# Second attention of a two-layer hybrid backbone: the next group's row maxima start seven score tiles after the group's start instead of four

## The chip, the cores and the metric

The kernel runs on one core of one Trainium2 chip. The metric is the device time of one execution in microseconds, lower is better. The profiles come from the hardware profiler, one execution each.

## The reference

The model is a two-layer backbone over 1024 latent tokens (a grid of 16 rows by 64 columns) and 256 context tokens, model width 1024, everything in fp32. Layer 0 has global and windowed attention. Layer 1, in which the change lies, has a convolution module and a neighbourhood attention with 8 heads of 64. Each query row of the grid sees the 256 context keys and a band of 8 rows by 16 columns, with a bias table for the relative position:

```python
bias = jnp.concatenate([ctx_open, bias], axis=-1)[None, :, None]
kk = jnp.concatenate([c_dk, kr], axis=1)
vv = jnp.concatenate([c_dv, vr], axis=1)
return gqa_attend(qr[:, :, :, None, :], kk, vv, bias).reshape(bsz, GRID_W, D_W)
```

`gqa_attend` is a softmax attention: scores, bias, softmax over the keys, product with the values. The result is gated with a SiLU, joined with the convolution's result, multiplied by an output matrix, added to the residual, and normalised.

## The kernel before

All matrix products are computed to nearly fp32 accuracy in three passes: each operand is split into a high part (`ph`, `wh`, `hh`) and a low part (`pl`, `wl`, `hl`); line 325 makes the high part (a cast on ACT), line 328 the low part (POOL or DVE), and lines 347 to 349 are the three matmuls.

The second attention handles 16 groups, g0 to g15. A group is one head and one half of the grid's columns, 512 queries. Heads 0 to 5 have their two halves one after the other; the last four groups are head 6 half 0, head 7 half 0, head 6 half 1, head 7 half 1. A group has seven score tiles: one of 128 context keys, five of the band (128 to 384 queries wide), and another of 128 context keys. Per tile:

- L503 and L507: two matmuls write the scores `st` (two PSUM banks). The first multiplies the queries' high part `QH` by the keys `KAt`; the second multiplies `QL` by `KBt`. Rows 64 to 67 of `QL` hold the negated row maxima of the four query blocks, so that the second matmul also subtracts the maximum.
- L512 (DVE) adds the bias `bs`, L513 (ACT) takes the exponential; for the context tiles L515 (ACT) does it alone. L325 and L328 split the result.
- L445 to L447: three matmuls, run three tiles later (`flush`), accumulate values and denominators in `ov`, of which there is one PSUM bank.

When the last tile of a group has been flushed, that is at tile 2 of the next group, DVE normalises: L455 (transpose), L457, L458, L1451 (`y` from `ov`; with it the bank is free) and L1453 (`y` times the gate). For heads 0 to 5 the result goes to DRAM (L1457), and comes back as `od` for the output projection; heads 6 and 7 stay on the chip.

Each group needs a preparation (`attn_prep`), a Python generator:

- its first step loads QH, QL and the bias for the maxima, `bm`, through SP's queue (L1382, L1383, L1385);
- six steps compute the row maxima: L1424 (matmuls against the context keys, two into one bank) with L1426 (a reduction on DVE), twice, and L1432 (a matmul against the band's keys) with L1435 (add the bias and take the maximum, on DVE), four times, in two banks `mx`;
- the seventh step reduces them (L405), two empty steps follow, and the tenth transposes the maxima (L415, PE) and writes them into QL (L416, DVE).

The first step of group g+2's preparation is taken at the first tile of g, and the rest is put into a list `work` with a due position, `x + LEAD[1]`, where x counts score tiles over all groups. From that position on, `prepare` takes `g.rate` = 3 steps a tile for each entry in the list, but only of the first entry while it lasts: half of them before the tile's flush, the rest after it. A dictionary changes the rule at the end: g11 takes up no preparation, g12 takes up those of g13 and g14, g13 that of g15. Before a group's first tile, whatever is left of its own preparation is run to its end:

```python
while any(p is g.prep for _, p in work):
    prepare(len(items), 1)
for k in g.ids:
    next(preps[k])
    work.append((x + LEAD[layer[0]], preps[k]))
```

The keys of the next head (`KAt`, 768 KB) are loaded through SP's queue at the start of a head's first half (L389), and ACT copies 64 of their rows to `KBt` at the end of that group (L593).

Beside the attention runs other matrix work, woven in as steps (`weave`): the projections of heads 4 to 7 (`d_proj`, matmuls `p`, whose results ACT and DVE evict, among them `vT`, `vc`, `sgd`, `spk`, `spq`, and `trv` are transposes of the values), then the output projection of the convolution's part (`po<-oc`), then that of the attention's part (`po<-od`), and the end of the kernel. These steps have a priority somewhat ahead of the attention's.

The order on each engine is then set by a planner: it simulates the program in time with costs of its own, and gives each engine, of the instructions that are ready in its simulation, the one that is first in the generators' order, corrected by the priorities. So an instruction that stands later may be placed earlier where an engine would have been free. On the chip each engine follows its list strictly in order.

Of the kernel before, what the change touches and what calls it, by code (L numbers as in the profile page):

```python
# [31 lines left out]
KROWS = ((0, 8), (0, 11), (4, 15), (8, 16))  # L32
BMO = (0, 320, 320, 760)
LOOK0, LOOK1 = 3, 3
LEAD = (3, 4)
AHEAD = 3
BSW, BMW = 768, 1080
CWB = 12
# [62 lines left out]
def tile_kernel(ctx: ExitStack, tc: tile.TileContext, a, out):  # L101
# [326 lines left out]
    def attn_gen(pool, groups, vshare, look, nexts=None):  # L428
# [58 lines left out]
        for x, (g, t) in enumerate(items):  # L487
            if x + AHEAD < len(items):
                items[x + AHEAD][0].ahead(items[x + AHEAD][1])
            if t == 0:  # L490
# [3 lines left out]
# [3 lines that stand above are left out]
            rate = g.rate * max(len(work), 1)  # L497
# [1305 lines left out]
```

## Time and profile before

| | |
|---|---|
| median of 3 runs | 1508.71 us (1506.60 to 1510.68) |
| profiled execution, its own time | 1508.76 us |
| span in its profile | 1506.7 us |
| mean granted TensorE clock | 0.977 |
| busy share: PE, weight loads, DVE, ACT, POOL | 95%, 77%, 72%, 50%, 54% |

The profile names engines as follows: PE is the matmul engine and PEld its weight loads, DVE the vector engine, ACT the activation engine, POOL GpSimd, SP the engine that issues most transfers. An instruction is shown by its start, its length, engine, line, operation, and output<-inputs. Square brackets hold the time in which the engine was idle before it, and what it waited for. A granted clock of 1.00 is full speed. In the second attention's stretch PE has the two longest waits at the row maxima of g4 and g8, whose queries are still on their way.

### The profile page before, as it was taken

Reading aid. Unit: us, or ns where it says so; the run is one execution under the profiler, and the core shown is the slowest. Engines: PE = TensorE matmul, PEld = TensorE weight load, DVE = VectorE, ACT = ScalarE, POOL = GpSimd, SP = SyncE. Lnnn points to the kernel's source line nnn. Section 1 sums busy time; section 2 is a strip of 40 time slices with the busy share of each in tenths; the row PEclk is TensorE's granted clock in tenths of the full one; section 3 lists DMA queues with packets and bytes.
Section 4 is the critical chain, followed back from the end, with each engine's and each line's share of the span. In section 5 each row is a group of like instructions: output and inputs, shape, how many; then the busy total and the mean of one; then the engine's idle time right before and its main releaser. Section 6 shows DMA issues by size and latency. Waiting matters only on the chain.

```text
span 1506.7 us, 22055 instructions
## 1 busy us (share of the span) xinstructions
PE 1424.8 (95%) x7006; PEld 1164.5 (77%) x7006; DVE 1086.2 (72%) x2139; ACT 750.3 (50%) x1536; POOL 816.9 (54%) x764
## 2 busy tenths in 40 slices
PE   7699999999999999999999989999999999999996
PEld 2598887987788678778888768888887878788775
DVE  5996787589957677555477676999938466677766
ACT  3541344446454765665455665443434354555563
POOL 3261463466555686776455765764543343364663
PEclk9799999999999999999999989999999999999998
DMA  9766245424541123641111122212596777797523
GB/s 351 261 201 190 73 123 179 144 67 122 161 133 47 45 84 119 218 156 45 49 42 43 60 77 80 86 65 69 160 315 197 209 219 209 231 292 219 189 63 119
DMA packets 182827, 215.23 MB, mean 143 GB/s; under 512 B 17196, under 2 KB 136184, under 8 KB 182712
## 3 DMA queue, kind: packets, MB, share of 16 engines
q1 hardware_dynamic: 176048, 202.26, 43.2%
q10 hardware_dynamic: 6664, 11.57, 2.4%
q8 instruction: 55, 0.90, 0.2%
q14 instruction: 60, 0.49, 0.1%
HBM read 151.64 MB, written 62.13 MB: 142 GB/s over the span
## 4 chain that ended last, share of the span: by engine, by line
PE 71%; DVE 13%; DMA 8%; issue 3%; POOL 2%; ACT 1%; SPq 1%; DVEq 0%; ACTq 0%; POOLq 0%
PE p L347 6%; PE p L348 6%; PE p L349 6%; PE ov L445 5%; PE ov L447 4%; PE ov L446 4%; PE po L347 4%; PE po L349 4%; PE po L348 4%; PE st L507 4%; PE st L503 4%; DMA mw<-in_mod_w_dram 3%; PE pg L347 2%; PE pq L349 2%; PE pq L347 2%
## 5 line engine op out<-in xcount | busy, mean ns | idle before, releaser
L328 POOL TENSOR_TENSOR pl<-pf,ph 128x512 fp32r<-128x512 f32 (+3 forms) x321 | 392.4, 1233 | 257.3 <-ACT ph L325 208.0
L328 POOL TENSOR_TENSOR wl<-wr,wh 128x256 fp32r<-128x256 f32 (+2 forms) x253 | 194.5, 787 | 160.5 <-ACT wh L325 112.4
L515 ACT ACTIVATE pf<-st 128x512 f32<-128x512 f32 x284 | 166.6, 596 | 179.6 <-PE st L507 129.9
L325 ACT CAST ph<-pf 128x512 fp32r<-128x512 f32 (+3 forms) x364 | 205.8, 578 | 24.0 <-PE ov L446 13.3
L347 PE MATMUL p<-hh,wh 128*128 128x512 f32 x448 | 177.6, 398 | 2.4 <-ACT wh L325 1.6
L348 PE MATMUL p<-hl,wh 128*128 128x512 f32 x448 | 178.0, 399 | 0.0
L349 PE MATMUL p<-hh,wl 128*128 128x512 f32 x448 | 173.1, 396 | 0.0
L325 ACT CAST wh<-wr 128x256 fp32r<-128x256 f32 (+2 forms) x260 | 101.6, 405 | 128.9 <-DMA wr<-in_od_d_dram 39.7
L445 PE MATMUL ov<-ph,Vt 128*128 128x512 f32 (+3 forms) x364 | 141.8, 390 | 10.1 <-DVE y L669 6.4
L503 PE MATMUL st<-QH,KAt 128*128 128x512 f32 (+3 forms) x364 | 139.7, 385 | 6.4 <-ACT pf L515 4.1
L447 PE MATMUL ov<-pl,Vt 128*128 128x512 f32 (+3 forms) x364 | 142.2, 392 | 3.7 <-DVE pl L328 1.9
L446 PE MATMUL ov<-ph,Vt 128*64 128x512 f32 (+3 forms) x364 | 139.5, 383 | 0.0
L507 PE MATMUL st<-QL,KBt 68*128 68x512 f32 (+3 forms) x364 | 135.6, 382 | 1.2 <-DVE QL L416 1.2
L1200 DVE SCALAR_TENSOR_TENSOR cps<-U,taps,cps 128x512 f32<-128x512 f32 x184 | 124.4, 749 | 0.1
L627 DVE TENSOR_REDUCE mp<-mx 128x1 f32<-128x512 f32 x128 | 85.6, 684 | 37.8 <-PE mx L626 37.1
L347 PEld LDWEIGHTS p<-hh,wh 128*128 128x128 f32 x448 | 84.5, 189 | 22.8 <-ACT wh L325 2.2
L349 PEld LDWEIGHTS p<-hh,wl 128*128 128x128 f32 x448 | 84.4, 188 | 20.1 <-issue 0.5
L348 PEld LDWEIGHTS p<-hl,wh 128*128 128x128 f32 x448 | 84.5, 189 | 19.0 <-issue 0.2
L447 PEld LDWEIGHTS ov<-pl,Vt 128*128 128x128 f32 x364 | 71.1, 195 | 27.6 <-POOL pl L328 5.1
L445 PEld LDWEIGHTS ov<-ph,Vt 128*128 128x128 f32 x364 | 71.4, 196 | 25.7 <-issue 6.1
L347 PE MATMUL pq<-wh,hh 128*128 128x384 f32 x256 | 88.0, 344 | 0.0
L349 PE MATMUL pq<-wh,hl 128*128 128x384 f32 x256 | 87.5, 342 | 0.0
(289 smaller groups left out, 3443.0 us busy)
## 6 DMA issues: line engine op xcount, KB each, us to landing
mw<-in_mod_w_dram SPq DMA_DIRECT2D x34, 512.0 KB, 5.9
Q<-qs SPq DMA_DIRECT2D x40, 256.0 KB, 2.6
QH<-Q SPq DMA_DIRECT2D x80, 128.0 KB, 2.8
bm<-in_d_bm_dram SPq DMA_DIRECT2D x16, 540.0 KB, 5.4
wr<-in_od_d_dram SPq DMA_DIRECT2D x64, 128.0 KB, 2.8
mw<-in_mod_w_dram SPq DMA_DIRECT2D x28, 256.0 KB, 3.0
wr<-in_ev_qkv_dram SPq DMA_DIRECT2D x32, 192.0 KB, 4.5
QD<-spq SPq DMA_DIRECT2D x48, 128.0 KB, 2.5
```

Source lines behind the costliest of these rows:

```text
L325: SC.copy(hi, src)
L328: (GP if leng == "g" else VE).tensor_tensor(lo, src, hi.bitcast(F32), op=ALU.subtract)
L347: PE.matmul(o, lh, rh, start=first, stop=False)
L348: PE.matmul(o, lh, rl, start=False, stop=False)
L349: done[0] = PE.matmul(o, ll, rh, start=False, stop=last)
L445: PE.matmul(o, V[:, 64:192], ph, start=(t == 0), stop=False)
L446: PE.matmul(cut(g.ov[0:64], q0, n), V[:, 0:64], ph, start=False, stop=False)
L447: pvs.append(PE.matmul(o, V[:, 64:192], pl, start=False, stop=(last and g.sink is None)))
L503: sts.append(PE.matmul(sf, KA[:, cs], cut(g.QH, q0, n), start=True, stop=False))
L507: PE.matmul(sf, KB[0:68, cs], cut(g.QL[0:68], q0, n), start=False, stop=True)
L515: SC.activation(pf[:, :n], st[:, :n], AF.Exp, scale=1.0 if g.bias else SCALE)
L1200: VE.scalar_tensor_tensor(pc, uc, w, pc, op0=ALU.mult, op1=ALU.add)
```

## The change

One constant: the second entry of `LEAD`, used in the second attention alone, goes from 4 to 7, the number of tiles in a group. The first attention's stays 3.

```diff
-LEAD = (3, 4)
+LEAD = (3, 7)
```

## Prediction before the run

> **What bounds the kernel now.** I read the page first, for the engines and the chain that ended last.
>
> ```profile
> span 1506.7 us, 22055 instructions
> PE 1424.8 (95%) x7006; PEld 1164.5 (77%) x7006; DVE 1086.2 (72%) x2139; ACT 750.3 (50%) x1536; POOL 816.9 (54%) x764
> PE 71%; DVE 13%; DMA 8%; issue 3%; POOL 2%; ACT 1%; SPq 1%; DVEq 0%; ACTq 0%; POOLq 0%
> ```
>
> PE is busy 95% of the span and holds 71% of the chain. The change adds and removes no instruction, so it can only pay by taking away or making idle time of PE (and the slow clock behind it). The stretch of the second attention, 1180 to 1440 us, by length and busy time (PE, its weight loads, DVE, ACT, POOL, then granted clock, DMA share and GB/s):
>
> ```profile
> 1180.00:1440.00 260.00, 246.01 (x1263) 206.28 (x1262) 179.64 (x443) 138.25 (x307) 123.69 (x141) 0.97 0.72 220
> ```
>
> PE idles 260.0 - 246.0 = 14 us of it; nothing larger than that is to be won by order alone, but for the clock. Next, PE in order of time: the idle in brackets stands ahead of the instruction. The rows are the two largest waits, what follows each, the start of some groups (g3 at 1236.52, g7 at 1315.35, g13 at 1412.91, g14 at 1431.83; g0 to g15 are the sixteen groups of seven tiles), and the late waits.
>
> ```profile
> 1228.16 0.47 PE L1424 MATMUL mx<-KAt,QH 128*128 128x256 f32 x2 [2.85 <-DMA QH<-QD]
> 1229.37 0.69 PE L1322 MATMUL trv<-ident,vc 128*128 128x128 f32 x2
> 1236.52 0.40 PE L503 MATMUL st<-QH,KAt 128*128 128x512 f32 x1
> 1296.93 0.71 PE L1424 MATMUL mx<-KAt,QH 128*128 128x256 f32 x2 [2.91 <-DMA QH<-QD]
> 1298.45 0.63 PE L347 MATMUL p<-hh,wh 128*128 128x512 f32 x1
> 1315.35 0.39 PE L503 MATMUL st<-QH,KAt 128*128 128x512 f32 x1
> 1389.41 0.47 PE L445 MATMUL ov<-ph,Vt 128*128 128x512 f32 x1 [0.61 <-DVE y L1451]
> 1412.91 0.40 PE L503 MATMUL st<-QH,KAt 128*128 128x512 f32 x1
> 1415.60 0.73 PE L347 MATMUL po<-od,wh 128*128 128x512 f32 x2 [1.14 <-ACT od L325]
> 1417.78 0.84 PE L507 MATMUL st<-QL,KBt 68*128 68x512 f32 x2
> 1425.45 0.40 PE L1424 MATMUL mx<-KAt,QH 128*128 128x256 f32 x2
> 1431.83 0.39 PE L503 MATMUL st<-QH,KAt 128*128 128x512 f32 x1
> 1437.10 0.69 PE L503 MATMUL st<-QH,KAt 128*128 128x384 f32 x1 [1.81 <-DVE pf L512]
> 1443.84 0.40 PE L507 MATMUL st<-QL,KBt 68*128 68x512 f32 x1
> ```
>
> Two waits of 2.85 and 2.91 us are row maxima, the moved step itself, whose queries QH have not landed. The chain that ended last passes through both transfers:
>
> ```profile
> 1220.25 7.78 DMA QH<-QD
> ...
> 1290.35 6.45 DMA QH<-QD
> ```
>
> The stretches around these waits and near the end of the attention, in the same columns:
>
> ```profile
> 1228.20:1232.00 3.80, 3.80 (x16) 3.39 (x17) 2.21 (x5) 2.73 (x8) 3.14 (x4) 0.57 1.06 389
> 1297.00:1302.00 5.00, 5.00 (x17) 4.26 (x18) 3.37 (x7) 3.32 (x8) 1.98 (x2) 0.66 1.05 334
> 1416.00:1420.00 4.00, 4.00 (x14) 3.23 (x13) 1.80 (x4) 2.13 (x6) 2.65 (x3) 0.57 0.73 245
> 1430.00:1441.00 11.00, 8.44 (x41) 6.69 (x39) 10.15 (x25) 6.68 (x16) 5.76 (x7) 0.82 0.37 113
> ```
>
> After each wait PE runs at about half clock for some microseconds, and the transfer engines are full. Who else waits there? ACT:
>
> ```profile
> 1226.55 1.47 ACT L593 CAST KBt<-KAt 64x1536 fp32r<-64x1536 f32 x1 [3.45 <-DMA KAt<-KD]
> 1228.97 0.35 ACT L1304 COPY vc<-p 128x256 f32<-128x256 f32 x1
> ...
> 1294.89 1.47 ACT L593 CAST KBt<-KAt 64x1536 fp32r<-64x1536 f32 x1 [4.20 <-DMA KAt<-KD]
> 1297.07 0.42 ACT L1309 COPY vT<-p 128x320 f32<-128x320 f32 x1
> ```
>
> This second waiter decides the size of the gain: ACT stands at the next head's keys, loaded with the same burst, until 1226.55 and 1294.89, then copies for 1.47 us, and only then come the exponentials and evictions that free PE's next work.
>
> **The change part by part.** The moved step holds, per group, these DVE instructions (busy, mean ns):
>
> ```profile
> L1435 DVE CUSTOM_DVE_ANT_0 mx<-mx,bm 128x440 f32<-128x440 f32 (+1 forms) x60 | 33.0, 560 | 22.9 <-PE mx L1432 22.4
> L1426 DVE TENSOR_REDUCE mp<-mx 128x2 f32<-128x512 f32 x29 | 19.8, 684 | 3.9 <-PE mx L1424 3.7
> L416 DVE TENSOR_TENSOR QL<-trn,k_bd 4x512 fp32r<-4x512 f32 x16 | 10.9, 682 | 0.5
> ```
>
> That is 4 x 0.560 + 2 x 0.684 + 0.682 = 4.3 us of DVE, and some short ones, beside eight maxima matmuls and one transpose on PE. It issues no DMA: the loads of QH, QL and the bias come at the group's first tile as before, so SP and POOL are moved past nothing, except that the bias load of g15 now waits for the maxima of g13 in SP's queue; behind it stands the gate load of g13, whose use is a group away, so I cost it at nothing.
>
> In the generator's order the ten calls of a preparation fell at tiles 4, 5 and 6 (three each) of group g and the last at tile 0 of g+1. With seven they start at tile 0 of g+1, where two preparations are queued and the rate is six: all six maxima calls at tile 0, the rest at tile 1. Around g11 and g12 it differs: g12 is prepared alone (three calls a tile, tiles 0 to 3 of g11), g13 falls due only when g13 itself starts, so its whole preparation is run ahead of its first score tile, and g15's runs over tiles 0 to 3 of g14.
>
> 1. Gain at the two waits. g4's maxima move from within g2 to g3's start, from 1228.16 to about 1236.5, and QH landed at 1220.25 + 7.78 = 1228.03; g8's move from 1296.93 to about 1315.4, landed at 1296.80. Both transfers are then early by 8 and 18 us. Gross this is 2.85 + 2.91 = 5.76 us, and the clock behind: 3.8 x 0.43 + 5.0 x 0.34 = 3.3 us; upper end 9.1. What is late next is ACT. At 1228 the work between the wait and the transpose (1229.37 - 1228.16 = 1.2 us) could run inside the gap, but the transpose needs vc, which ACT ends at 1229.32. At 1297 the work until the projection (1298.45 - 1296.93 = 1.5 us) fits in the gap, but the projection needs a bank that the vT copy frees at 1297.49, so it comes some 1.0 us earlier. Lower end 1.2 + 1.0 = 2.2. I take -4.0, nearer the lower end, since ACT's rows are the nearer ones and the gap that stays keeps the slow clock.
>
> 2. Gain at g11's result. DVE's order in g12:
>
> ```profile
> 1406.38 0.62 DVE L1435 CUSTOM_DVE_ANT_0 mx<-mx,bm 128x440 f32<-128x440 f32 x1
> ...
> 1407.03 0.69 DVE L1426 TENSOR_REDUCE mp<-mx 128x2 f32<-128x512 f32 x1
> 1407.75 1.78 DVE L1453 SCALAR_TENSOR_TENSOR y<-y,gt 64x512 f32<-64x512 f32 x1
> ```
>
> g13's maxima stand between the pieces of g11's result y, 1407.75 - 1406.38 = 1.37 us of them right ahead of its last one. That result goes to DRAM and back as od, for which PE idles 1.14 us at 1415.60, then runs four microseconds at 0.57, 1.7 us lost. Without them: 0 to -2.9. I take -1.1, the wait alone, because g13's maxima may still be fetched forward.
>
> 3. g13's bunched preparation.
>
> ```profile
> 1414.42 0.68 DVE L416 TENSOR_TENSOR QL<-trn,k_bd 4x512 fp32r<-4x512 f32 x1
> ...
> 1434.64 0.68 DVE L416 TENSOR_TENSOR QL<-trn,k_bd 4x512 fp32r<-4x512 f32 x1
> ```
>
> Before, g13's maxima row was written by 1415.10, and the first score that needs it ran at 1417.78. The quickest nearby preparation is g15's, from 1425.45 to 1435.32: 9.9 us. Begun only at g13's first score (1412.91), it ends at 1422.8, 5.0 us after 1417.78. But the planner fetches work forward where an engine is free, so with DVE's 4.3 us alone it would be in time. 0 to +5.0; I take +1.5.
>
> 4. g15. Its preparation takes 9.9 us, and g14, in which it now lies, has from 1431.83 to 1443.84, where g15's row is needed: it just fits. But DVE is busy 10.15 of 11 us there and PE already waits 1.81 us for it; two maxima operations that ran before 1430 come in, 0.68 + 0.56 = 1.2 us. 0 to +3.0 (they come in, and the 1.81 is had once more); I take +1.0, near the 1.2.
>
> 5. The crowd at the start of a group. The 4.3 us of DVE now stand at tiles 0 and 1, right ahead of the previous group's normalisation at tile 2, which frees the one ov bank. One wait for it stands in the trace, 0.61 us at 1389.41. Over 13 boundaries 0 to +7.9, and below nothing by that 0.61 if the old place was its cause. I take +1.0.
>
> Sum: -4.0 - 1.1 + 1.5 + 1.0 + 1.0 = -1.6. The profiled execution took 1508.76 us (span 1506.7 and 2.1 around it), beside a median of 1508.71, so the time comes to 1507.1.
>
> Term 1 rests on the clock. The rows show half clock after waits of 2.85 and 2.91 us. "TensorE: Matmul & The Clock Gate", Part 1, of the Trainium skill has the clock halve after at least one idle window of about 3.4 us; by its length alone these gaps would cost no clock, the upper end of term 1 would be 5.76 and the sum no other, since I take 4.0. The rows of this case disagree with that reading and decide.
>
> **The rivals.** A: the planner, with the maxima out of the way, lays other ready work under the key loads, and both gaps go with their slow clock: -9.1 in place of -4.0, so 1508.8 - 9.1 - 1.1 + 3.5 = 1502.1. For it: PE has projection work right behind (1298.45). Against: ACT's own wait remains. B: the ov bank. The crowd delays the normalisation at every boundary as at 1389.41: +7.9 in place of +1.0, 1514.0, slower. It decides from 0.55 us a boundary: 13 x 0.55 = 7.1 in place of +1.0 puts the sum above +4.5. Against: DVE is free 28% of the span. C: g13's row is late by the full 5.0 us and the clock falls, 1.7 more as after the wait at 1415.60: 1507.1 + 5.2 = 1512.3, about at the bound. D: the planner's forward fetching puts the maxima back near their old place, and the time stays 1508.7.
>
> **How the numbers follow.** A difference under 0.3% (4.5 us) can't be told from none here. Forecast and D together 0.39, A 0.34, B 0.15, C 0.12. A ends under 1504.2, B above 1513.2, C half above it: faster 0.34, same 0.39 + 0.06 = 0.45, slower 0.21; as a new order can draw a new stall of the size of those seen (2.9 us and its clock, twice), I move 0.06 from same to slower. The range goes from 1499.5 (A without the 3.5 of terms 3 to 5 would be 1498.6) to 1514.0 (B). The likeliest case's own range is 1504 to 1511.
>
> **What would show it.** Step 1: no row-maxima matmul waits for QH; ACT still waits for the keys at L593, and PE has shorter gaps at the same places. Step 2: g11's y ends earlier against g12's first score and PE's wait for od shrinks. Step 3: a wait on QL or its transpose ahead of g13's scores. Step 4: more than 1.81 us of PE waits for DVE in g14. Step 5: more waits of ov for y. The prediction is wrong if the gaps at the key loads vanish altogether, or if the score tiles from g12 on are stretched by more than 5 us.

## The result and the profile after

The changed kernel is slower: 1514.16 us at the median against 1507.35 us for the kernel before in the same session, a ratio of 1.0037 [1.0020, 1.0053]. Two repeats gave 1.0036 [1.0015, 1.0057] and 1.0037 [1.0022, 1.0052]. The forecast was no change, 1507.1 us. The profile shown here is that of the first repeat (its own time 1515.06 us), as the execution that was profiled with the first result ran at about half the granted clock throughout. Its page:

```profile
span 1513.3 us, 22060 instructions
...
PE 1425.0 (94%) x7006; PEld 1161.3 (77%) x7006; DVE 1086.3 (72%) x2139; ACT 749.2 (50%) x1536; POOL 814.6 (54%) x764
...
PE 71%; DVE 11%; DMA 10%; issue 3%; POOL 2%; ACT 2%; SPq 1%; ACTq 0%; DVEq 0%; POOLq 0%
```

Over the whole span PE is busy as long as before (1424.8 us), and the span is 6.6 us longer. In the chain that ended last, transfers go from 8% to 10%. PE in order of time, the waits of the changed kernel and two rows of the output projection (the idle in brackets stands ahead of the instruction):

```profile
1226.82 0.48 PE L1424 MATMUL mx<-KAt,QH 128*128 128x256 f32 x2 [2.20 <-DMA QH<-QD]
1296.78 0.77 PE L1424 MATMUL mx<-KAt,QH 128*128 128x256 f32 x2 [2.96 <-DMA QH<-QD]
1328.78 0.50 PE L347 MATMUL po<-oc,wh 128*128 128x512 f32 x1 [2.22 <-ACT wh L325]
1356.73 0.48 PE L1424 MATMUL mx<-KAt,QH 128*128 128x256 f32 x2 [0.90 <-DMA QH<-QD]
1401.52 0.47 PE L1424 MATMUL mx<-KAt,QH 128*128 128x256 f32 x2 [1.17 <-DMA KAt<-KD]
1403.43 0.39 PE L503 MATMUL st<-QH,KAt 128*128 128x256 f32 x1 [0.71 <-ACT pf L515]
1421.48 0.39 PE L503 MATMUL st<-QH,KAt 128*128 128x256 f32 x1 [0.91 <-ACT pf L515]
1424.70 1.05 PE L347 MATMUL po<-od,wh 128*128 128x512 f32 x2
1444.22 0.44 PE L503 MATMUL st<-QH,KAt 128*128 128x384 f32 x1 [1.34 <-DVE pf L512]
```

The two waits for QH that the change was to remove are both still there. The order of the matmuls says why: it is that of before, instruction by instruction, up to g6's first maxima, in tile 3 of g4. In score tiles ahead of a group's own first tile (its first and last maxima against the band's keys, L1432, and its transpose, L415):

| group | before | changed |
|---|---|---|
| g4 | 11/8/6 | 11/8/6 |
| g6, g7 | 11/7/5, 12/8/6 | 11/7/4, 12/7/5 |
| g8 | 13/8/6 | 9/5/2 |
| g9, g12 | 13/9/7, 11/7/5 | 11/8/5, 11/7/4 |
| g13, g14, g15 | 5/1/0, 8/6/3, 11/6/5 | 7/3/1, 8/6/5, 12/11/9 |

The planner fetches the preparation forward to wherever an engine is free, so a due position three tiles later changes nothing for the preparations of g2 to g5. It redraws two later stretches: g6 to g11, and g12 to the end.

To say where the time is lost, I take score tiles at which both orders have run exactly the same matmuls: g6.1 (group 6, tile 1), g9.3, g11.4 and g15.6. Between them, before and then changed (length, then the engines' busy times, granted clock, DMA share, GB/s):

```profile
1292.81:1354.96 62.15, 57.63 (x300) 48.47 (x299) 43.67 (x104) 36.76 (x81) 27.80 (x32) 0.97 0.85 265
1354.96:1388.29 33.33, 33.09 (x168) 27.18 (x166) 26.83 (x71) 17.70 (x38) 17.12 (x20) 1.00 0.75 232
1388.29:1460.98 72.69, 67.95 (x323) 55.84 (x321) 52.74 (x117) 43.68 (x94) 45.30 (x49) 0.93 0.44 137
```

```profile
1292.59:1358.91 66.32, 60.23 (x301) 50.40 (x299) 43.84 (x106) 35.93 (x78) 28.34 (x32) 0.92 0.81 253
1358.91:1392.00 33.09, 32.68 (x168) 27.10 (x166) 25.48 (x69) 17.57 (x38) 15.89 (x19) 1.00 0.73 213
1392.00:1467.53 75.53, 68.64 (x323) 54.73 (x322) 53.66 (x117) 42.27 (x94) 44.75 (x49) 0.95 0.43 135
```

The first stretch is 4.17 us longer: PE is busy 2.60 us longer for the same matmuls, at a clock of 0.92 in place of 0.97, and idles 1.57 us more. The last is 2.84 us longer. What lies between is nearly the same. One execution of one order scatters by some microseconds, so each stretch is read below from several.

### The profile page after: what moved, and what is told of

Read it like the earlier page. It is cut to its first block, busy times and chain, and to the rows that moved or that the text cites. A ratio compares the mean times of both kernels' runs of the same rounds, so it can differ in the third digit from the quotient of the medians.

```text
span 2315.7 us, 22060 instructions
## 1 busy us (share of the span) xinstructions
PE 2277.9 (98%) x7006; PEld 1463.6 (63%) x7006; DVE 1070.6 (46%) x2139; ACT 758.8 (33%) x1536; POOL 796.2 (34%) x764
## 4 chain that ended last, share of the span: by engine, by line
PE 97%; DVE 2%; issue 0%; DMA 0%; ACT 0%; POOL 0%; DVEq 0%; SPq 0%; ACTq 0%; POOLq 0%
PE p L349 8%; PE p L348 8%; PE p L347 8%; PE ov L445 5%; PE ov L446 5%; PE ov L447 5%; PE st L503 5%; PE st L507 5%; PE po L347 5%; PE po L348 5%; PE po L349 5%; PE pq L349 4%; PE pq L347 4%; PE pq L348 4%; PE pg L348 3%; PE pg L347 3%
## 5 line engine op out<-in xcount | busy, mean ns | idle before, releaser
L348 PE MATMUL p<-hl,wh 128*128 128x512 f32 x448 | 259.0, 580 | 0.0
L347 PE MATMUL p<-hh,wh 128*128 128x512 f32 x448 | 258.2, 578 | 0.5 <-ACT vc L1304 0.5
L349 PE MATMUL p<-hh,wl 128*128 128x512 f32 x448 | 254.8, 580 | 0.0
L503 PE MATMUL st<-QH,KAt 128*128 128x512 f32 (+3 forms) x364 | 199.0, 548 | 1.7 <-DVE pf L512 1.3
L445 PE MATMUL ov<-ph,Vt 128*128 128x512 f32 (+3 forms) x364 | 197.0, 541 | 3.6 <-DVE y L669 1.8
L447 PE MATMUL ov<-pl,Vt 128*128 128x512 f32 (+3 forms) x364 | 197.2, 542 | 2.9 <-DVE pl L328 1.9
L446 PE MATMUL ov<-ph,Vt 128*64 128x512 f32 (+3 forms) x364 | 197.3, 542 | 0.0
L507 PE MATMUL st<-QL,KBt 68*128 68x512 f32 (+3 forms) x364 | 193.6, 542 | 0.0
L349 PE MATMUL pq<-wh,hl 128*128 128x384 f32 x256 | 125.1, 489 | 0.0
L348 PE MATMUL pq<-wl,hh 128*128 128x384 f32 x256 | 122.2, 477 | 0.0
```

Source lines behind the costliest of these rows:

```text
L347: PE.matmul(o, lh, rh, start=first, stop=False)
L348: PE.matmul(o, lh, rl, start=False, stop=False)
L349: done[0] = PE.matmul(o, ll, rh, start=False, stop=last)
L445: PE.matmul(o, V[:, 64:192], ph, start=(t == 0), stop=False)
L446: PE.matmul(cut(g.ov[0:64], q0, n), V[:, 0:64], ph, start=False, stop=False)
L447: pvs.append(PE.matmul(o, V[:, 64:192], pl, start=False, stop=(last and g.sink is None)))
```

## The experiments

My theories, with letters of their own (the rivals A to D of the prediction are others), each stated before the runs that test it: D, any redrawn order costs, whichever it is; M, what costs is that maxima come later (they shorten the reserve of every wait behind them); T, it is the order of the last groups from g13; F, the planner's forward fetching keeps the maxima at the QH waits and so hides a gain; C, maxima and the previous group's result crowd on DVE at a group's start. "Kernel" stands for the kernel before with the edit named. All ratios are to the kernel before on the same chip, with 95% intervals.

**Where in the list.** The changed kernel again; the end with the old lead; the end alone with the new.

```diff
 # again7: LEAD = (3, 7)
 # late4: lead 7, but 4 for g13 to g15
-work.append((x + LEAD[layer[0]], preps[k]))
+work.append((x + (4 if layer[0] and k >= 13 else LEAD[layer[0]]), preps[k]))
 # late7: lead 4, but 7 for g13 to g15
+work.append((x + (7 if layer[0] and k >= 13 else LEAD[layer[0]]), preps[k]))
```

> The changed kernel itself, for a profile at full clock. Both theories expect the slowdown measured before, 3 to 8 us over the kernel before. Theory T (tail): until g12's first tile its trace is level with or ahead of before's, and the loss stands between g12's first tile and the end of the attention. Theory C (crowd): the loss is spread over the groups from g1 on, as waits of PE for the ov bank or for DVE.

> Lead seven for the preparations up to g12, four for g13, g14 and g15. T: the slowdown is gone, 0 to 9 us faster than before, since the gain at the two waits for queries stays and the bunch ahead of g13 is undone. C: still 3 to 8 us slower than before.

> Lead four for the preparations up to g12, seven for g13, g14 and g15: the bunch alone. T: 3 to 10 us slower than before. C: within 2 us of before. The two waits for queries, 2.85 and 2.91 us, stand in both.

Measured: 1.0036 [1.0015, 1.0057], 1.0027 [1.0010, 1.0044] and 1.0000 [0.9985, 1.0014]. late4's order turned out to be the changed kernel's on all five engines, so it is a further repeat of it and not the test it was meant to be. late7's is that of before up to g13's preparation, and level, so T, which expected 3 to 10 us from it, falls. The due positions of g13 to g15 do nothing much by themselves; their order in the changed kernel follows from g12's, as a later run shows.

**How much lead.** One size changed: `LEAD = (3, n)`.

> Lead five for all: each preparation starts one tile later than before and still ends before its group, with no bunch ahead of g13. T: within 3 us of before or faster. C: about a third of the slowdown, 1 to 3 us slower.

> Lead one: the preparations are due earlier, and in PE's list the transposed maxima of g6 to g12 stand 6.1 tiles ahead of their group on average (before 5.6, changed kernel 4.3). Theory M (later maxima cost, earlier ones don't): within 2 us of before or faster. Theory D (any redrawn order costs, since the order before is a good draw): 2 to 6 us slower.

> Lead three: the lists are those of before until g8, with small differences behind (transposed maxima 5.7 tiles ahead on average). M: within 2 us of before or faster. D: 1 to 5 us slower.

> Lead six: transposed maxima 4.9 tiles ahead on average, g8's four tiles ahead (before six, changed kernel two). M: between lead five (same as before) and the changed kernel, 1 to 4 us slower. D: 2 to 6 us slower, with no order among the leads.

> Lead nine: transposed maxima 4.0 tiles ahead on average, those of g7 only at its own start. M: as slow as the changed kernel or slower, 4 to 9 us. D: 2 to 6 us slower.

Measured, for 1, 3, 5, 6, 7 (again7) and 9 tiles: 0.9995 [0.9982, 1.0008], 0.9995 [0.9982, 1.0009], 1.0005 [0.9991, 1.0018], 1.0017 [1.0003, 1.0032], 1.0036, 1.0034 [1.0021, 1.0046]. Leads 1 and 3 redraw the order too and cost nothing, so D falls. M fits: 6 lies between, 7 and 9 cost the whole, though the intervals of 6 and 7 overlap.

**The order as the change was meant.** A later preparation step is made to wait for the score matmul issued last, so that the planner can't fetch it forward; once with lead 7, once with lead 4.

```diff
-                if next(work[0][1], work) is work:
-                    work.pop(0)
+                with tc.issue_after(sts[-1].ins) if layer[0] and sts else nullcontext(): r = next(work[0][1], work)
+                if r is work: work.pop(0)
```

> Lead seven, and each later step of a preparation of the second attention is also made to wait for the score matmul last issued, so the planner can't fetch it forward: the preparations stand in PE's list at tiles 0 to 4 of the group before, as the change's text says. Theory F (the planner's forward fetching undid the change; the two waits for queries are still there and would be worth something if they went): no row maxima wait for QH, 2 to 9 us faster than before. Theory C (the crowd at a group's start costs): slower than before by 3 us or more, with waits for the ov bank or for DVE in the place of those for QH.

> The same hold with lead four: the maxima stand at tiles 4 to 6, where the generators put them, and not at tile 2 or 3. F: the waits for QH shrink, 0 to 5 us faster than before. C: within 2 us of before, since nothing is crowded at a group's start.

Measured: held7 1.0061 [1.0049, 1.0074], held4 1.0018 [1.0006, 1.0029]; 1516.23 us and 1508.61 us at the median, 7.6 us apart, with 1507.02 us for the kernel before on the same chip. In both the maxima do move, and no row-maxima matmul waits for QH. The first maxima of g4 and g8 in held4, without a bracket:

```profile
1223.49 0.40 PE L1424 MATMUL mx<-KAt,QH 128*128 128x256 f32 x2
1299.09 0.41 PE L1424 MATMUL mx<-KAt,QH 128*128 128x256 f32 x2
```

The same two in held7, and two of the waits that came instead:

```profile
1233.89 0.40 PE L1424 MATMUL mx<-KAt,QH 128*128 128x256 f32 x2
1312.69 0.40 PE L1424 MATMUL mx<-KAt,QH 128*128 128x256 f32 x2
1308.99 0.50 PE L445 MATMUL ov<-ph,Vt 128*128 128x512 f32 x1 [1.39 <-DVE y L1451]
1322.71 0.58 PE L503 MATMUL st<-QH,KAt 128*128 128x256 f32 x1 [3.60 <-ACT pf L515]
```

So F is half right: forward fetching does keep the maxima in place, but it hides no net gain, and held4, which has neither QH wait, is no faster either. Put where the due positions say, the maxima leave the QH waits. In held7 PE then waits for `ov`'s bank (by y, L1451; twice, 2.9 us in all), for ACT's `pf` (4.7 us) and for DVE's (4.6 us), as C said; in held4 it is never for `ov`, and 2.5 us for each of the other two.

**Which of the two stretches.** Lead 7 for the preparations up to g8; for g9 to g12; for g12, g10 or g8 alone.

```diff
-work.append((x + LEAD[layer[0]], preps[k]))
+work.append((x + (7 if layer[0] and k <= 8 else LEAD[layer[0]]), preps[k]))  # k2_8, middle2, middle3
+work.append((x + (7 if layer[0] and 9 <= k <= 12 else LEAD[layer[0]]), preps[k]))  # k9_12
+work.append((x + (7 if layer[0] and k == 12 else LEAD[layer[0]]), preps[k]))  # tail; only10, only8 with 10 and 8
```

> Lead seven for the preparations up to g8, four behind: the list of every engine is that of the changed kernel until g9, and another from there. Theory E (the loss comes from the new order in g6 to g9): 3 to 6 us slower than before. Theory L (it comes from the new order of g10 to g12 and behind): within 2 us of before.

> Lead seven for g9 to g12 alone: the lists are those of before until g9, and from g12 on PE's order of the preparations is that of the changed kernel. E: within 2 us of before. L: 3 to 6 us slower than before.

Measured: 1.0023 [1.0008, 1.0038] and 1.0031 [1.0019, 1.0042], so neither E nor L alone. The second was the outlier: its maxima for g11 and g12 come earlier than before, against M, and its end has the changed kernel's order.

> Lead seven for g12's preparation alone. The matmul list is that of before as far as g10, and from there to the end, but for a few swaps, that of the changed kernel: g13's, g14's and g15's maxima stand where the change puts them (transposes 1, 5 and 9 tiles ahead of their own group, before 0, 3 and 6). Sum theory (the cost of the change is that of its two redrawn stretches added, g6 to g11 and g12 to the end): 1.0036 less the 1.0023 of the kernel with the first stretch alone, so 1.0010 to 1.0018, +2 us. Theory 'tail' (the end's order is what costs, which the kernel with lead seven for g9 to g12 hints at): 1.0025 to 1.0035, +4 to +5 us. Theory 'late' (only maxima that come later cost, and here none come later): 0.9990 to 1.0008.

> Lead seven for g10's preparation alone. It shares with the kernel of lead seven for g9 to g12 the order from g9 to g11 (the transposes of g11 and g12 stand one and two tiles earlier than before), and has the end's order of before. If that kernel's +0.31% is the end's order, this one is level: 0.9990 to 1.0008. If it is the order from g9 to g11, then 1.0020 to 1.0035, +3 to +5 us, and the theory that only later maxima cost falls. If both add: about 1.0015.

> Lead seven for the preparations up to g8, once more, as the share of the first redrawn stretch (g6 to g11, with g8's transpose at 2 tiles ahead of its group, before 6) rests on one interval of 1.0008 to 1.0038. Its list is the changed kernel's as far as g10 and before's after it, but for swaps in the last 150 rows. Theory 'late': 1.0025 to 1.0038, all of the change's cost. Sum theory: 1.0015 to 1.0025, with the rest found at the end. Theory 'tail': 1.0000 to 1.0012.

> Lead seven for g8's preparation alone: its last maxima stand 6 and its transpose 2 tiles ahead of g8, before 8 and 6, while g10's and g11's stand about a tile earlier, and the end's order is that of before. Theory 'late' and the chain by the bias buffers (g8's last maxima free the buffer late, the next bias load goes out directly ahead of the output weights, and the matmul engine waits for these): 1.0015 to 1.0030, +2 to +4.5 us, with a wait of over 1 us for the weights' high part near g7's start. If it is not g8's lateness: 0.9990 to 1.0008, and no such wait.

> Lead seven for the preparations up to g8 a third time, now on the same chip as the changed kernel, because two measurements of it gave 1.0023 and 0.9999. If the cost lies in the first redrawn stretch: as the changed kernel, 1.0030 to 1.0040. If it is spread over both stretches: 1.0005 to 1.0020, 2 to 4 us under the changed kernel. If the first stretch costs nothing: 0.9990 to 1.0005.

> The changed kernel once more, beside the one with its first redrawn stretch alone. It measured 1.0037, 1.0036 and (as an equal list under another rule) 1.0027. Expected 1.0025 to 1.0040; if the two stretches' costs of about 0.1% each are simply added, 1.0020. Below 1.0015 the cost of the change itself would be in doubt.

Measured: tail 1.0010 [0.9996, 1.0024], only10 1.0025 [1.0012, 1.0038], middle2 0.9999 [0.9986, 1.0011], only8 1.0008 [0.9993, 1.0023], middle3 1.0003 [0.9986, 1.0021], whole3 1.0037. By their own expectations tail gives what the sum theory gave it, middle2 and middle3 say that the first stretch costs next to nothing, and only8 that g8's lateness is not the cause. The three measurements of the first stretch alone average (0.23 - 0.01 + 0.03) / 3 = 0.08%; on one chip, the whole and the first stretch alone are 1513.42 and 1507.38 us. By the medians neither half carries the cost, and their sum, 0.18%, falls short of the whole, though their intervals are wide enough to make it up. The traces show more. Each figure is the time between two L503 rows at which all these kernels have run the same matmuls; the last column runs to the span's end, which is given to 0.1 us. A row is one profiled execution, and whole3's and middle3's are 2.5 and 3.4 us above their kernels' medians:

| execution (order) | g6.1 to g9.3 | g9.3 to g11.4 | g11.4 to g15.6 | to the end |
|---|---|---|---|---|
| before | 62.15 | 33.33 | 72.69 | 45.72 |
| late7 (before's to g13) | 64.88 | 34.06 | 70.78 | 45.78 |
| tail (before's, changed end) | 61.57 | 33.10 | 73.77 | 45.76 |
| again7 (changed) | 66.32 | 33.09 | 75.53 | 45.77 |
| late4 (changed) | 66.19 | 34.09 | 73.18 | 45.48 |
| whole3 (changed) | 66.46 | 32.43 | 74.96 | 45.29 |
| k2_8 (changed first stretch) | 64.40 | 33.83 | 73.23 | 44.60 |
| middle2 (the same) | 64.72 | 32.79 | 73.15 | 44.59 |
| middle3 (the same) | 64.39 | 32.93 | 71.21 | 44.53 |
| only10 (a third order in g9 to g11) | 63.79 | 38.49 | 72.41 | 45.73 |
| k9_12 (that order, changed end) | 62.47 | 37.68 | 72.22 | 45.74 |

First column: the changed order 65.4 on average of six, the old one 63.0 of five (only10 and k9_12 leave it at g8.2): +2.4 us, and all but late7's 64.88 lie apart. A kernel of yet another order, lead3, warns that this is not far beyond the scatter: it is level by its median, and took 64.85 us here in its profiled execution, the longest of its twelve. Third column: the changed end 73.9 of five, before's 72.5 of five (late7 left out, as its end is of neither order): +1.4 us, but the two groups overlap (72.22 against 73.23). Fourth: the kernels with the first stretch alone happen to get another order of the output stage, 1.2 us shorter than before, which hides half of what the first stretch costs them. So tail should cost 1.4 us, and has 1.5 (0.10%); the first stretch 2.4 - 0.3 - 1.2 = 0.9 us, and has 1.2 (0.08%); the whole 2.4 - 0.3 + 1.4 - 0.2 = 3.3 of some 5.3 measured. With the whole's own three executions the first column is 66.3 and the third 74.6, and it comes to 3.3 - 0.3 + 2.0 - 0.2 = 4.8; with their own three the kernels of the first stretch alone come to 1.5 - 0.3 - 1.2 = 0. So the table shows where the time goes, and not to the microsecond. Why the whole's order is 1.8 us longer in the first stretch than the same matmul order in the kernels of that stretch alone stays open; part of it is a further block of half clock (below), and with three executions each it may be scatter.

**What happens in the first stretch.** g8's maxima end 3 tiles later than before. The `bm` they read occupies one of two buffers, so the next `bm`, 540 KB, goes out later. SP's issues, changed:

```profile
1320.47 0.41 SPq L1385 DMA_DIRECT2D bm<-in_d_bm_dram  x1
1321.37 2.42 SPq L358 DMA_DIRECT2D wr<-in_od_wo_dram  x3
```

and before, where the bias load goes out 7 us ahead of the next output weights:

```profile
1315.28 0.33 SPq L1385 DMA_DIRECT2D bm<-in_d_bm_dram  x1
...
1322.55 1.19 SPq L358 DMA_DIRECT2D wr<-in_od_wo_dram  x2
```

The weights now travel right behind the bias. The changed kernel's chain that ended last (start, length, what):

```profile
1320.61 0.74 POOL wl L328
...
1321.37 6.93 DMA wr<-in_od_wo_dram
...
1328.33 0.41 ACT wh L325
...
1328.78 0.50 PE po L347
```

Then the clock falls, to 0.68 over 5.3 us. In shorter windows it is half clock for 3.41 us, with full clock on either side (the columns are those of the stretches above):

```profile
1328.70:1334.00 5.30, 5.22 (x20) 4.46 (x21) 1.59 (x4) 3.10 (x10) 3.14 (x4) 0.68 0.76 224
1326.80:1330.21 3.41, 1.43 (x8) 1.15 (x8) 2.54 (x6) 1.04 (x3) 0.88 (x2) 1.00 0.92 321
1330.21:1333.62 3.41, 3.41 (x14) 3.02 (x12) 0.85 (x1) 2.05 (x6) 2.26 (x3) 0.50 0.75 206
1333.62:1337.04 3.42, 3.42 (x17) 2.76 (x17) 1.42 (x4) 1.29 (x4) 2.67 (x3) 1.00 0.86 269
```

In the second attention of all these traces half clock comes in such blocks, of 3.41 us or twice that, and in one execution they start whole multiples of 3.41 us apart: before's at 1228.72, 1296.99 and 1416.45, 20 and 35 of them. In the 3.41 us ahead of these PE idled 1.98 us here, and 2.85 and 2.91 us ahead of before's first two; the wait of 0.90 us at 1356.73 is followed by no such block. So what a wait costs seems to depend on its length and on where it falls. Counting a double block as two, the first stretch holds one in four of the five executions of the old order (clock 0.97) and two in only10 (0.95), two in each kernel of the first stretch alone (0.95), and three in each of the whole (0.92 to 0.94).

The same wait for `wh` stands in four of the six executions of this order, and where it doesn't, g11's first maxima wait for their queries some 25 us on. One row each of whole3, k2_8, late4 and middle2:

```profile
1330.40 0.79 PE L347 MATMUL po<-oc,wh 128*128 128x512 f32 x1 [2.97 <-ACT wh L325]
```

```profile
1328.45 0.80 PE L347 MATMUL po<-oc,wh 128*128 128x512 f32 x1 [2.64 <-ACT wh L325]
```

```profile
1354.79 0.48 PE L1424 MATMUL mx<-KAt,QH 128*128 128x256 f32 x2 [2.30 <-DMA QH<-QD]
```

```profile
1352.40 0.51 PE L1424 MATMUL mx<-KAt,QH 128*128 128x256 f32 x2 [2.57 <-DMA QH<-QD]
```

In the five executions of the old order neither wait exceeds 0.31 us. It is not the start of the weights' load that is late: by the chain above it went out when POOL had made the low part (`wl`) from the weights before them, and so freed their buffer, 1.2 us earlier than in the kernel before. It takes longer. From the issue to the cast that waits for it pass 3.0 to 3.3 us in the five executions of the old order, where `bm` went out 7 to 9 us ahead, and 4.4 to 7.7 us in the six of the changed one, where it went out 0.9 to 2.4 us ahead. only8, the test of this chain, warns against calling the buffer the whole cause: there too `bm` goes out right ahead of the weights (1318.19 and 1318.97) and they take 6.1 us, but no matmul waits for `wh`, and the kernel is level. What the runs show is the place and the two late transfers; that the bias load delays the weights fits these twelve executions and was not tried by itself.

**The outlier.** only10's +5 us in the second column has its own cause. Its ACT, the same cast before, and the same in k9_12:

```profile
1355.57 0.62 ACT L325 CAST od<-od 128x512 fp32r<-128x512 f32 x1 [5.50 <-DMA od<-O1d]
```

```profile
1352.87 0.62 ACT L325 CAST od<-od 128x512 fp32r<-128x512 f32 x1 [2.18 <-DMA od<-O1d]
```

```profile
1354.53 0.62 ACT L325 CAST od<-od 128x512 fp32r<-128x512 f32 x1 [4.55 <-DMA od<-O1d]
```

ACT stands 5.50 us (4.55 in k9_12) at a result on its way through DRAM, and the exponentials and casts behind it in its list come late; in only10 DVE idles 6.42 us for such a cast at 1356.76, and then adds the next bias. PE of only10 and of k9_12 pays at the next score:

```profile
1358.07 0.44 PE L503 MATMUL st<-QH,KAt 128*128 128x384 f32 x1 [2.26 <-DVE pf L512]
```

```profile
1357.03 0.44 PE L503 MATMUL st<-QH,KAt 128*128 128x384 f32 x1 [1.44 <-DVE pf L512]
```

Over that stretch PE idles 3.2 us in each of the two, where it idled 0.2 us before. The changed kernel's own order has no such loss there (33.2 against 33.5 us). So k9_12 measured 1.0031 for a reason that the changed kernel doesn't share, and M holds only as "later maxima cost where a transfer depends on them", not as "earlier is safe".

No version was measurably faster than the kernel before.

## Why the prediction was wrong

1. The failed step is the first: "g4's maxima move from within g2 to g3's start" and g8's to about 1315.4. They did not: the list is the same up to g6's first maxima, g4's stay where they were, and g8's first maxima (L1424) still stand within g6, at the key load. Of the -4.0 us nothing came; the waits of 2.85 and 2.91 are 2.20 and 2.96. In place of the gain came a loss of 0.37%, which the table puts into the two stretches that the planner redrew: late transfers and the half clock behind them from g6 to g11, and more waits at the end. Nor is it shown that moving them would pay: held4 and held7 have neither wait and are 0.18% and 0.61% slower. I had read where the generator puts the steps, though the planner sets the order. I used its forward fetching to excuse term 3 and to price rival D, and did not apply it to step 1.
2. Term 2, -1.1, came in kind, by another way than I gave. The wait for od is gone in all five executions with the changed end, and there, at 1.06 to 1.18 us, in the five with the old one. Middle2 and tail:

```profile
1416.55 0.73 PE L347 MATMUL po<-od,wh 128*128 128x512 f32 x2 [1.06 <-ACT od L325]
```

```profile
1417.97 1.05 PE L347 MATMUL po<-od,wh 128*128 128x512 f32 x2
```

   But y was not earlier. In the changed kernel its last piece starts at

```profile
1413.65 1.23 DVE L1453 SCALAR_TENSOR_TENSOR y<-y,gt 64x512 f32<-64x512 f32 x1
```

   15.7 us after g12's first score (1397.97), where before it was 12.5 us (1407.75 and 1395.25). The projection itself was put later, at 1424.70 in place of 1415.60.
3. Term 3, +1.5: no bunch. g13's maxima were fetched forward into g12, earlier than before (7/3/1 against 5/1/0). In the profile shown they met the key load of the next head, 1.17 us at 1401.52, which I had not priced; the other four executions with this end have no such wait.
4. Term 4, +1.0, "more than 1.81 us of PE waits for DVE in g14": it is 1.34. With terms 2 and 3, the end as a whole cost +1.4 us, where I had -1.1 + 1.5 + 1.0 = +1.4. The sum agrees by chance: its parts were not right, and the measured +1.4 is within the scatter.
5. Term 5, +1.0: not in the changed order, as the maxima don't stand at the groups' starts. held7 shows that the mechanism exists, at two boundaries with 2.9 us in all; its 7.6 us over held4 lie near rival B's +7.9 by chance, since it also waits longer for ACT and DVE.
6. The coupling by the bias buffers I saw only for g15 and cost at nothing. It acted at g8, where output weights stand behind it, and is a likely source of the +2.4 us of the first stretch, though only8 speaks against it as the only one.

Rival D had the mechanism right and the result wrong: the place stays where the waits are, and the list is redrawn further on. A had no ground, since held7 and held4 moved the maxima and gained nothing net. Rival B's 1514.0 us is almost the 1514.16 measured, but by chance: in the changed kernel PE waits once for `ov` by y in the whole attention, 0.41 us. Rival C did not occur. The 0.06 that I moved to "slower" for "a new stall of the size of those seen (2.9 us and its clock, twice)" describes what happened in the first stretch, once in each execution of the new order (at 1328.78 in the profile shown, at 1354.79 in late4); it deserved a case of its own with a place and a price.

On the clock, the wait of 2.22 us at 1328.78 and the half clock behind it agree with the rows of before, not with the reading of the Trainium skill's "TensorE: Matmul & The Clock Gate", Part 1, that about 3.4 us of idling come first. The same page of the Trainium skill says there that the window runs freely. The blocks of 3.41 us on one grid agree with that, and 1.98 us of idling within 3.41 were enough here. For the weights, the Trainium skill's "DMA: Bandwidth & Descriptors", section "Anatomy of one DMA", gives a fit of 2.0 us plus the bytes over 436 GB/s for GpSimd's path, which makes an estimate of 2.3 us for 128 KB. This transfer through SP's queue took 6.93 us in a burst.

## What to carry to other kernels

Where a planner sets the order, the first question on a moved due position is which instructions will stand elsewhere, and it is answered by comparing the two instruction lists, not the generators: here the two waits that I priced stayed where they were, and the list changed from g6 to g11, where I had not looked, and at the end. For each operation whose place moves, follow the buffer that it frees to the transfer that waits for it, and then to whatever stands behind that transfer in its queue. And compare two orders between points at which both have done the same work, over several executions: the 2.4 us of the first stretch showed in that table, if not far beyond the scatter, while the medians of the halves were level.

## What the runs showed that I had not expected

- The lead doesn't act evenly: 1 to 5 tiles lie within 0.1% of each other, 7 and 9 cost 0.34% to 0.37%.
- Equal instruction lists on two chips gave 1.0023 [1.0008, 1.0038] and 0.9999 [0.9986, 1.0011] against the kernel before on each, and 1.0003 on a third. The intervals tell the scatter within a session, and something more has to be allowed between sessions.
- The clock behind a wait can cost more than the wait: of the first stretch's 4.17 us in the profiled pair, 2.60 are busy time for the same matmuls, with three blocks of half clock in place of one.
